# In the hybrid trunk, the second tiles of two forms of the pooled channels follow bank evictions on VectorE

## The chip, the cores and the metric

The kernel runs on one NeuronCore of a Trainium2 chip. The metric is the device time of one execution in microseconds (us); lower is better. TensorE (PE) multiplies matrices into the banks of PSUM, VectorE (DVE) and ScalarE (ACT) read the banks and work on tiles in SBUF, GpSimd (POOL) works on SBUF alone, and SyncE (SP), ScalarE and GpSimd issue DMAs. Each engine takes its own queue of instructions in a fixed order.

## The reference

One layer of a streaming encoder over 2048 positions of 1024 channels, and a final norm. What matters here is the first half of the layer:

```
xn = rmsnorm(x, norm1_g)
z  = xn @ w_in          # u_pool | q | f | i | o | branch gates
gates = sigmoid(zg + b_gate)                      # two of 1024 channels
ya = pool_mixer(u_pool, pool_w, pool_scale) @ w_pa    # 512 -> 1024 channels
yb = hgrn2_mixer(zq, zf, zi, zo, ...) @ w_pb          # a gated recurrence, 4 heads
merged = gates[0] * ya + gates[1] * yb
x = x + merged @ w_o
x = x + conv_glu_ffn(rmsnorm(x, norm2_g), ...)
out = rmsnorm(x, final_g)
```

The pool mixer takes trailing means over windows of 2, 4, 8 and 16 positions, multiplies each group of 128 channels by a matrix of its own and scales the result; these are the "pooled channels" that w_pa multiplies.

## The kernel before

**Passes and blocks.** The sequence is worked off in two passes of 1024 positions. A pass has a mixer (the projections, the pool mixer, the recurrence, the merge) and a feed-forward part. It works on two blocks of 512 positions at once, so that a tile has 128 channels and 512 positions.

**Seven products for eight.** Each large product is cut in a two by two manner: two halves of the contraction, two blocks of positions, two tiles of output channels. The eight partial products are made from seven (P1 to P7) by a Strassen-Winograd scheme. It multiplies sums of weights by sums of inputs. The sums of inputs are called forms: B11, B21, B22, T1 to T4. The table `FORM` says which product uses which: P1 B11, P6 T2, P5 T1, P7 T3, P2 B21, P4 T4, P3 B22, and `ORDER` is the order P1, P6, P5, P7, P2, P4, P3.

**Hi and lo.** Every operand is split into a high part (a cast on ScalarE) and a low part (what is left, a subtraction on VectorE), and each product is made of three matmuls: high by high, high by low, low by high. For weights this is done by the stream (lines 231 and 232), a few operands ahead of the products; for the forms by `split` (lines 659 and 660).

**A unit and its banks.** A `Unit` makes two output tiles for both blocks with three PSUM banks, X, Z and V. P1 and P2 add into X, P6, P7 and P4 into Z, P5 and P3 into V. Between two products of a bank its content has to be read: after P6 VectorE computes u2 from bank Z (line 1200), after P7 it computes u3 from bank Z (line 1204) and an output from bank V. P7's products can start only when u2 has read the bank, and P4's only when u3 has. `after("P6")` and `after("P7")` hand u2 and u3 to `first`, which remembers the latest of them. `second(ins)` puts an instruction behind the remembered one in the order of their engine; so far only the convolution of the feed-forward part uses it.

**The order of the work.** The Python program issues the matmuls in order. After every sixth matmul comes a tick, at which waiting tasks (generators) go on: the stream of weights, the four heads of the recurrence, the pool mixer and others. `yield n` waits n ticks. A planner then fixes the order of each engine's queue ahead of the run, from the program's order, from the dependencies and from estimated times; `in_turn` tells it that an instruction comes after the last matmul issued, `behind` that it comes after another instruction of its engine. Neither makes an engine wait for another engine on the chip.

**The pooled forms.** The mixer's last projection unit is the unit of gates 7 (tiles `gr_...` in the profile). Behind it come the products of the pooled channels with w_pa (tiles `pa_...`): two rounds d = 0, 1, in each of which two units (e = 0, 1) share the weights of a product, first all of unit 0's matmuls, then all of unit 1's. A form of the pooled channels has two tiles, j = 0 and 1 (two groups of 128 channels). `pa_task` (line 1460 on) makes them, paced by the counter `place`: it counts up behind each product of the last gate unit (1 after P1, 2 after P6, 3 after P5, 4 after P7 ... 7 after P3), and ahead of each product of the pooled units (8 at P1, 9 at P6, 10 at P5, 11 at P7, 12 at P2, 13 at P4, 14 at P3 of round 0). A product has twelve matmuls, so two ticks.

In `pa_task`, `minus` subtracts two tiles (line 1477), `form` splits the result. T2 (with t1 and t2, `mf_t` in the profile, and the parts `mf0T20h` to `mf0T21l` in the first pass) is issued from place 3 on, tile 0 at one tick and tile 1 at the next, both while P7 of the last gate unit is issued. T3's subtractions run on GpSimd, from place 5. T4 is issued from place 8, behind B21, tile 0 at one tick and tile 1 at the next, while P6 of the pooled units is issued. B22 (a negated copy on ScalarE, line 1519, and its split) is issued from place 10. In between, the heads of the recurrence issue `ss` and `st` (line 1118), `ot` (line 1139) on VectorE and `pv`, `po`, `pt` on TensorE.

Of the kernel before, what the change touches and what calls it, by code (L numbers as in the profile page):

```python
# [15 lines left out]
ALU = mybir.AluOpType  # L16
# [65 lines left out]
def tile_trunk(  # L82
# [26 lines left out]
    def slot(name, cols=TB, dt=F32):  # L109
        return slots.tile([P, cols], dt, tag="s", name=name, padded_shape=[P, 528])  # L110
# [148 lines left out]
    def behind(ins, other):  # L259

        tc.add_manual_dep(ins.ins, other.ins.name, mybir.DependencyInfo(
            mybir.DependencyClass.NoSync, mybir.DependencyReason.DATA), reason="behind")
# [7 lines left out]
    def second(ins):  # L270
        if urgent[0] is not None:
            behind(ins, urgent[0])
        return ins

    def in_turn(ins):

        tc.add_manual_dep(ins.ins, count[1].ins.name, mybir.DependencyInfo(
            mybir.DependencyClass.NoSync, mybir.DependencyReason.SCHED_ONLY), reason="in turn")

    stream = Stream()  # L280

    class Sums:
# [12 lines left out]
        def make(self, g):  # L295
            n = len(self.groups[g][0])
            for k in ("s1", "s2", "s3", "s4"):
                nm = f"{self.name}{g}{k}"
                self.t[g, k] = dram.tile([P, n, 512], F32, tag=nm, name=nm)
            for dst, src, add in (("s1", 2, 0), ("s3", 2, 0), ("s1", 3, 1), ("s3", 0, 1),  # L300
                                  ("s2", "s1", 0), ("s2", 0, 1), ("s4", "s2", 0), ("s4", 1, 1)):
                x = self.t[g, src] if isinstance(src, str) else self.groups[g][1][src]
                if add:
                    in_turn(pool.dma_start(self.t[g, dst], x, accum_op=ALU.add))
                else:
                    with tc.issue_after(stream.mark.ins):
                        act.dma_start(self.t[g, dst], x)
                yield SUM_LAG
            self.done.add(g)
# [343 lines left out]
    def split(src, name, on_pool=False):  # L653
        hi = slot(name + "h", TB, F32R)
        lo = slot(name + "l", TB, F32R)
        if on_pool:
            up = pool.tensor_scalar(hi, src, 1.0, 0.0, ALU.mult, ALU.add)
        else:
            up = act.copy(hi, src)
        low = dve.tensor_tensor(lo, src, f32(hi), ALU.subtract)  # L660
        last_split[0] = up, low
        return hi, lo
# [297 lines left out]
    def fetch(d, name, eng=sp):  # L960
        t = slot(name)
        eng.dma_start(t, d)  # L962
        return t


    def hgrn_task(b, h, d, q, vd, zd, od):
# [27 lines left out]
        def two_levels(hh):  # L994
# [27 lines left out]
            for i in range(0, NT, 2):  # L1022
                cc = slice(i, i + 2)
                mv = mvs[i]
                pa_ = bank(f"pl{b}_{h}_{hh}_{i}", 384)
                for c in range(2):
                    ins = pe.matmul(pa_[:, c * 192 : c * 192 + 192],  # L1027
                                    ks[:, (i + c) * P : (i + c + 1) * P],
                                    mv[:, c].rearrange("p s x -> p (s x)"),
                                    start=True, stop=True)  # L1030
                    if not (i or c):
                        in_turn(ins)
                ps = pa_.rearrange("p (c s x) -> p c s x", c=2, s=3)
                yield 1
                dve.copy_predicated(av[:, cc, :, 1, :], mask(hh, 2),
                                    ps[:, :, 0].rearrange("p c (b h) -> p c b h", h=hh))
                for t in range(2):
                    dve.copy_predicated(av2[:, cc, :, 1, :], mask(8 * hh + 1 - t, 2),
                                        ps[:, :, 1 + t].rearrange("p c (b h) -> p c b h", h=2 * hh))
# [12 lines left out]
        for lv in (0, 1, 2, 4, 6):  # L1052
# [7 lines left out]
            if lv < 2:  # L1060
                qd, ad = ((q1, ae), (q2, ao))[lv]
                if lv == 1:
                    act.copy(q2[:, :, 0].rearrange("p c (b h) -> p c b h", h=2), qv[:, :, :, 1, :])
                    yield AHEAD
                pa_ = bank(f"pl{b}_{h}_{hh}")
                for c in range(NT):
                    ins = pe.matmul(pa_[:, c * P : (c + 1) * P], ks[:, c * P : (c + 1) * P],
                                    qd[:, c].rearrange("p s x -> p (s x)"),
                                    start=True, stop=True)
                    if not c:  # L1070
                        in_turn(ins)
                yield 2
                pv4 = pa_.rearrange("p (c s x) -> p c s x", c=NT, s=2)
                dve.copy_predicated(ad, masks[-1 - lv].to_broadcast([P, NT, 64]), pv4[:, :, 1])
                pv4 = pv4[:, :, 0].rearrange("p c (b h) -> p c b h", h=hh)
            else:
                yield AHEAD
                pa_ = bank(f"pl{b}_{h}_{hh}", 256)
                for c in range(NT):
                    ins = pe.matmul(pa_[:hh, c * hh : (c + 1) * hh], ks[:, c * P : c * P + hh],  # L1080
                                    qv[:, c, 0, 1, :], start=True, stop=True)
                    if not c:
                        in_turn(ins)
                yield 2
                act.copy(av[:hh, :, 0, 1, :], pa_[:hh].rearrange("p (c h) -> p c h", c=NT))
# [285 lines left out]
    def mixer(b0, forms, late):  # L1371
# [90 lines left out]
        place = [0]  # L1462

        def pa_task():
            t = {}
            for hf, g in ((0, 0), (0, 1), (1, 0), (1, 2), (1, 1), (1, 3), (0, 2), (0, 3)):
                while (b0 + hf, g) not in md:
                    yield 1
                t[hf, g] = fetch(md[b0 + hf, g], f"mx{b0 + hf}_{g}")

            def form(key, j, x):
                pf[key].append(split(x, f"mf{b0}{key}{j}"))
                in_turn(last_split[0][0])

            def minus(key, j, x0, x1, eng=dve):
                x = slot(f"mf{b0}_{key}{j}")
                in_turn(eng.tensor_tensor(x, x0, x1, ALU.subtract))
                return x

            while place[0] < 2:  # L1480
                yield 1
            for j in range(2):
                form("B11", j, t[0, j])
                yield 1
            t1, t2 = [], []
            while place[0] < 3:
                yield 1
            for j in range(2):
                t1.append(minus("t1", j, t[1, j], t[0, j]))
                t2.append(minus("t2", j, t[1, j + 2], t1[j]))  # L1490
                form("T2", j, t2[j])
                yield 1
            while place[0] < 5:
                yield 1
            t3 = [minus("t3", j, t[1, j], t[1, j + 2], pool) for j in range(2)]
            for j in range(2):
                form("T1", j, t1[j])
                yield 1
            while place[0] < 6:
                yield 1  # L1500
            for j in range(2):
                form("T3", j, t3[j])
                yield 1
            while place[0] < 7:
                yield 1
            for j in range(2):
                form("B21", j, t[0, j + 2])
                yield 1
            while place[0] < 8:
                yield 1  # L1510
            for j in range(2):
                t4 = minus("t4", j, t[0, j + 2], t2[j])
                form("T4", j, t4)
                yield 1
            while place[0] < 10:
                yield 1
            for j in range(2):
                x = slot(f"mf{b0}_b22{j}")
                in_turn(act.activation(x, t[1, j + 2], AF.Copy, scale=-1.0))
                form("B22", j, x)  # L1520
                yield 1
# [3 lines left out]
        for n, (kind, i) in enumerate(PROJ):  # L1525
            if (kind, i) == ("u", 0):
                held["w"] = stream.get("pw")
            u = Unit(f"{kind[0]}r{b0}_{i}", "in", emits[kind](i))
            for p in ORDER:
                u.multiply(p, forms, late)  # L1530
                u.after(p)
                if n == len(PROJ) - 1:
                    if p == "P1":
                        quiet[0] = True
                        mtask = Task(pa_task())
                    place[0] += 1
# [437 lines left out]
```

## Time and profile before

| | before |
|---|---|
| median of 3 runs | 2515.26 us (2512.67 to 2516.94) |
| the profiled execution | 2514.4 us |
| its span, first to last instruction | 2512.7 us |
| mean granted clock of TensorE | 0.998 |
| TensorE busy, matmuls / weight loads | 2494.6 us / 2048.8 us |
| VectorE, ScalarE, GpSimd busy | 1996.1 / 1214.1 / 808.3 us |

In a timeline a row has the start and the duration in us, the engine, the line of the kernel, the operation, the tiles as out<-in, the shape and a count. Behind it, in brackets, is how long the engine had been idle and what released it. In the waits a row has the waiting engine and line, what it waited for, and then the total in us, the number of times and the longest. A view of windows has, for each stretch, its length, the busy time and count of PE, PEld, DVE, ACT and POOL, then the granted clock of TensorE, the share of the DMA engines and GB/s. The first pass's last gate unit and first pooled units lie at about 425 to 470 us, the second pass's at 1665 to 1715 us.

### The profile page before, as it was taken

How to read it: one execution, taken by the hardware profiler on the slowest of the kernel's cores; microseconds unless marked ns; L12 is line 12 of the kernel's file. 1: busy time of each engine (PE TensorE's matmuls, PEld its weight loads, DVE VectorE, ACT ScalarE, POOL GpSimd, SP SyncE). 2: the span in 40 equal slices, each digit the busy share in tenths (PEclk: the TensorE clock that was granted, in tenths of full speed). 3: DMA queues.
4: the chain of work that ended last, by engine and by line, in shares of the span. 5: the costliest groups of instructions: out<-in, count | busy, mean ns of one | idle time of the engine just before them, and what ended most of it. 6: DMA issues, size and time to landing. Idle time of an engine off the chain costs nothing.

```text
span 2512.7 us, 35696 instructions
## 1 busy us (share of the span) xinstructions
PE 2494.6 (99%) x11460; PEld 2048.8 (82%) x11460; DVE 1996.1 (79%) x3528; ACT 1214.1 (48%) x2286; POOL 808.3 (32%) x1139
## 2 busy tenths in 40 slices
PE   9999999999999999999999999999999999999998
PEld 7888888788888888888888888887888888888887
DVE  7788878897998778885596778778979888778755
ACT  5534443435555445553554434443355555445534
POOL 4343453403344333551320202123033433325410
PEclk9999999999999999999999999999999999999999
DMA  8877787687888789897344343446443444447852
GB/s 271 273 200 221 214 219 225 216 241 248 208 249 243 221 228 247 264 366 234 114 158 152 106 134 110 143 151 238 132 155 121 153 150 139 150 135 245 322 165 99
DMA packets 252332, 493.76 MB, mean 197 GB/s; under 512 B 26544, under 2 KB 43056, under 8 KB 251824
## 3 DMA queue, kind: packets, MB, share of 16 engines
q1 hardware_dynamic: 184512, 313.60, 38.4%
q0 software_dynamic: 42656, 112.74, 17.7%
q10 hardware_dynamic: 24976, 65.13, 7.5%
q8 instruction: 91, 1.49, 0.2%
q14 instruction: 97, 0.79, 0.1%
HBM read 381.79 MB, written 187.17 MB: 226 GB/s over the span
## 4 chain that ended last, share of the span: by engine, by line
PE 98%; DVE 1%; ACT 1%; DMA 0%; issue 0%; POOL 0%; SPq 0%; ACTq 0%
PE dn_P L148 17%; PE up_Z L148 15%; PE up_X L148 10%; PE up_V L148 10%; PE wo_P L148 6%; PE gr_Z L148 5%; PE gr_V L148 4%; PE pb L148 4%; PE gr_X L148 3%; PE io_Z L148 3%; PE fr_Z L148 3%; PE fr_V L148 2%; PE fr_X L148 2%; PE io_V L148 2%; PE pl L1027 2%; PE ur_Z L148 1%
## 5 line engine op out<-in xcount | busy, mean ns | idle before, releaser
L231 ACT CAST ops<-raw 128x512 fp32r<-128x512 f32 x794 | 490.1, 620 | 842.9 <-PE dn_P L148 176.4
L232 DVE TENSOR_TENSOR ops<-raw,ops 128x512 fp32r<-128x512 f32 x794 | 596.4, 755 | 206.2 <-ACT ops L231 199.4
L1705 DVE SCALAR_TENSOR_TENSOR e<-h,cols,e 128x512 f32<-128x512 f32 x176 | 141.4, 808 | 30.8 <-ACT e L1703 23.7
L1703 ACT ACTIVATE e<-h,cols 128x512 f32<-128x512 f32 x176 | 142.2, 814 | 25.6 <-DVE h L1160 18.3
L1708 DVE SCALAR_TENSOR_TENSOR e<-h,cols,e 128x512 f32<-128x512 f32 x176 | 134.9, 776 | 2.5
L962 POOL DMA_DIRECT2D g_P<-dg_P x154 | 83.7, 545 | 161.5 <-PE dn_P L148 111.6
L1273 POOL TENSOR_TENSOR gf_P<-e,e 128x512 f32<-128x512 f32 x44 | 61.7, 1403 | 150.2 <-DVE e L1714 95.9
L446 POOL TENSOR_TENSOR raw<-raw,raw 128x512 f32<-128x512 f32 x36 | 50.6, 1405 | 150.5 <-DVE ops L232 136.6
L1273 POOL TENSOR_TENSOR gf_P<-gf_P,e 128x512 f32<-128x512 f32 x44 | 59.2, 1345 | 71.7 <-DVE e L1714 71.2
L1698 POOL COPY h<-h 128x2 f32<-128x2 f32 x88 | 39.8, 465 | 117.7 <-DVE h L1159 110.9
L1413 POOL TENSOR_TENSOR q<-q,qs 128x512 f32<-128x512 f32 x16 | 21.8, 1363 | 167.5 <-ACT qs L1412 167.5
L1712 ACT ACTIVATE e<-e 128x512 f32<-128x512 f32 x88 | 55.6, 632 | 40.2 <-DVE e L1708 39.8
L1700 POOL COPY hist<-h 128x2 f32<-128x2 f32 x88 | 35.1, 398 | 116.7 <-DVE h L1160 114.7
L1160 DVE TENSOR_TENSOR h<-up_u,up_V 128x512 f32<-128x512 f32 x88 | 60.1, 683 | 10.2 <-PE up_V L148 9.7
L1248 DVE TENSOR_TENSOR x<-x,wo_P 128x512 f32<-128x512 f32 x88 | 55.9, 688 | 9.0 <-PE wo_P L148 8.6
L1248 DVE TENSOR_TENSOR ac<-ac,dn_P 128x512 f32<-128x512 f32 x72 | 47.2, 683 | 16.1 <-PE dn_P L148 15.8
L1012 POOL COPY qm<-q 128x64 f32<-128x64 f32 x64 | 26.6, 436 | 100.9 <-DVE q L1044 20.8
L1450 ACT ACTIVATE gt<-gt,cols 128x512 f32<-128x512 f32 x48 | 34.8, 725 | 49.9 <-DVE gt L1160 40.5
L1198 ACT COPY up_e<-up_X 128x512 f32<-128x512 f32 x44 | 25.8, 586 | 57.0 <-PE up_X L148 49.8
L1728 POOL DMA_DIRECT2D dg_P<-gf_P x88 | 50.7, 576 | 8.3 <-POOL gf_P L1273 7.4
L1698 POOL COPY h<-hist 128x2 f32<-128x2 f32 x88 | 44.4, 512 | 27.3 <-issue 14.8
L1027 PE MATMUL pl<-qm,k 128*128 128x192 f32 x256 | 50.2, 326 | 0.0
(1364 smaller groups left out, 8106.4 us busy)
## 6 DMA issues: line engine op xcount, KB each, us to landing
g_P<-dg_P POOLq DMA_DIRECT2D x154, 256.0 KB, 6.2
raw<-in_w_up_t SPq DMA_DIRECT2D x132, 256.0 KB, 3.2
raw<-in_w_in_t SPq DMA_DIRECT2D x98, 256.0 KB, 3.4
dg_P<-gf_P POOLq DMA_DIRECT2D x88, 256.0 KB, 3.9
dg_P<-e SPq DMA_DIRECT2D x66, 256.0 KB, 3.6
raw<-in_w_dn SPq DMA_DIRECT2D x66, 256.0 KB, 3.8
x<-in_x SPq DMA_DIRECT2D x64, 256.0 KB, 5.0
gd<-gt ACTq DMA_DIRECT2D x64, 256.0 KB, 3.0
```

The costliest lines, as they stand in the source:

```text
L148: count[1] = pe.matmul(*args, **kw)
L231: self.mark = act.copy(hi, v)
L232: low = self.low = dve.tensor_tensor(lo, v, f32(hi), ALU.subtract)
L962: eng.dma_start(t, d)
L1027: ins = pe.matmul(pa_[:, c * 192 : c * 192 + 192], ks[:, (i + c) * P : (i + c + 1) * P], mv[:, c].rearrange("p s x -> p (s x)"), start=Tru ...
L1160: return dve.tensor_tensor(dst, t, ps, ALU.add if how == "add" else ALU.subtract)
L1248: dve.tensor_tensor(t, t, ps[j], ALU.add if sg > 0 else ALU.subtract)
L1273: pin(eng.tensor_tensor(t, x0, x1, op))
L1698: pool.tensor_copy(h[:, 0:2], hist[:, mt] if hf == 0 else hs[s, 0][:, TB : TB + 2])
L1703: in_turn(act.activation(t, h[:, 2:], AF.Identity, bias=col(o_cb + mt), scale=col(o_cw + 4 * MF + mt)))
L1705: in_turn(second(dve.scalar_tensor_tensor(t, h[:, 1 : 1 + TB], col(o_cw + 2 * MF + mt), t, ALU.mult, ALU.add)))
L1708: dve.scalar_tensor_tensor(t, h[:, 0:TB], col(o_cw + mt), t, ALU.mult, ALU.add)
```

## The change

`in_turn` now returns its instruction. `minus` puts the second tile (j = 1) of t1 and of t4 behind the remembered eviction with `second`. The waits for a place become a helper, `reach`. The second tile of T2 (t1, t2 and the split) is issued at place 4 instead of 3, when u3 of the last gate unit is the remembered eviction. The second tile of T4 is issued at place 10, where it was issued one tick behind the first from place 8 on; the remembered eviction is then u2 of the pooled unit 1 in round 0. B22 is issued from place 11 instead of 10. T1, T3, B21, B11 and all first tiles keep their places. No instruction is added or taken away.

```diff
@@ def in_turn(ins)
         tc.add_manual_dep(ins.ins, count[1].ins.name, ...)
+        return ins
@@ def pa_task()
             def minus(key, j, x0, x1, eng=dve):
                 x = slot(f"mf{b0}_{key}{j}")
-                in_turn(eng.tensor_tensor(x, x0, x1, ALU.subtract))
+                ins = in_turn(eng.tensor_tensor(x, x0, x1, ALU.subtract))
+                if j and key in ("t1", "t4"):
+                    second(ins)
                 return x
 
-            while place[0] < 2:
-                yield 1
+            def reach(n):
+                while place[0] < n:
+                    yield 1
+
+            yield from reach(2)
...
             t1, t2 = [], []
-            while place[0] < 3:
-                yield 1
             for j in range(2):
+                yield from reach(3 + j)
                 t1.append(minus("t1", j, t[1, j], t[0, j]))
                 t2.append(minus("t2", j, t[1, j + 2], t1[j]))
                 form("T2", j, t2[j])
                 yield 1
...
-            while place[0] < 8:
-                yield 1
             for j in range(2):
+                yield from reach(8 + 2 * j)
                 t4 = minus("t4", j, t[0, j + 2], t2[j])
                 form("T4", j, t4)
                 yield 1
-            while place[0] < 10:
-                yield 1
+            yield from reach(11)
             for j in range(2):
                 x = slot(f"mf{b0}_b22{j}")
                 in_turn(act.activation(x, t[1, j + 2], AF.Copy, scale=-1.0))
```

More of the change, by code (lines that the diff above doesn't have):

```diff
@@ L1492, in pa_task @@
                 yield 1
-            while place[0] < 5:
-                yield 1
+            yield from reach(5)
             t3 = [minus("t3", j, t[1, j], t[1, j + 2], pool) for j in range(2)]
@@ L1498, in pa_task @@
                 yield 1
-            while place[0] < 6:
-                yield 1
+            yield from reach(6)
             for j in range(2):
@@ L1503, in pa_task @@
                 yield 1
-            while place[0] < 7:
-                yield 1
+            yield from reach(7)
             for j in range(2):
@@ L1508, in pa_task @@
                 yield 1
-            while place[0] < 8:
-                yield 1
             for j in range(2):
+                yield from reach(8 + 2 * j)
                 t4 = minus("t4", j, t[0, j + 2], t2[j])
@@ L1514, in pa_task @@
                 yield 1
-            while place[0] < 10:
-                yield 1
+            yield from reach(11)
             for j in range(2):
```

## The prediction

> **What bounds the kernel now.** I read the page first, then the waits of TensorE and of its weight loads, then the timelines of the stretches in which those waits lie. The page:
>
> ```profile
> span 2512.7 us, 35696 instructions
> PE 2494.6 (99%) x11460; PEld 2048.8 (82%) x11460; DVE 1996.1 (79%) x3528; ACT 1214.1 (48%) x2286; POOL 808.3 (32%) x1139
> PE 98%; DVE 1%; ACT 1%; DMA 0%; issue 0%; POOL 0%; SPq 0%; ACTq 0%
> ```
>
> TensorE carries 98% of the chain that ended last. Some 18 us of the span have no matmul in them (2512.7 - 2494.6), so a change that takes no matmul out can win no more than that and what slow matmuls cost. Where the holes are, the waits of TensorE say, and the same waits as its weight loads see them:
>
> ```profile
> PE pa_Z L148 <- DVE pa_u L1200: 4.1, 2, 2.1
> PE gr_Z L148 <- DVE gr_u L1204: 1.9, 2, 1.0
> ```
> ```profile
> PEld pa_Z L148 <- DVE pa_u L1200: 4.6, 2, 2.3
> PEld gr_Z L148 <- DVE gr_u L1204: 2.3, 2, 1.2
> ```
>
> Columns: total us, times, longest. Each wait occurs twice, once in each of the two passes over the sequence. In both, products into bank Z wait until VectorE has read that bank (u3 of the last gate unit, u2 of the second pooled unit). The timeline of VectorE in the first pass shows what stands ahead of u3:
>
> ```profile
> 434.64 1.03 DVE L660 TENSOR_TENSOR mf0T20l<-mf_t,mf0T20h 128x512 fp32r<-128x512 f32 x1 [0.43 <-ACT mf0T20h L659]
> 435.60 0.68 DVE L1477 TENSOR_TENSOR mf_t<-mx,mx 128x512 f32<-128x512 f32 x1
> 436.31 0.69 DVE L1477 TENSOR_TENSOR mf_t<-mx,mf_t 128x512 f32<-128x512 f32 x1
> 437.69 0.69 DVE L660 TENSOR_TENSOR mf0T21l<-mf_t,mf0T21h 128x512 fp32r<-128x512 f32 x1 [0.68 <-ACT mf0T21h L659]
> 438.30 0.68 DVE L1204 TENSOR_TENSOR gr_u<-gr_Z,gr_e 128x512 f32<-128x512 f32 x1
> ```
>
> The three instructions between T2's first low part and u3 are t1, t2 and the low part of the second tile, with a hole of 0.68 in which VectorE waits for the cast on ScalarE. TensorE beside it: the last product that u3 needs, and the wait.
>
> ```profile
> 432.69 0.39 PE L148 MATMUL gr_Z<-x_T33h,ops 128*128 128x512 f32 x1
> 439.04 0.50 PE L148 MATMUL gr_Z<-x_T40h,ops 128*128 128x512 f32 x1 [0.95 <-DVE gr_u L1204]
> ```
>
> u3's input was there at 433.1; it started 5.2 us later. The second place, VectorE and then TensorE:
>
> ```profile
> 452.86 0.68 DVE L660 TENSOR_TENSOR mf0T40l<-mf_t,mf0T40h 128x512 fp32r<-128x512 f32 x1
> 453.46 0.68 DVE L1200 TENSOR_TENSOR pa_u<-pa_e,pa_Z 128x512 f32<-128x512 f32 x1
> 454.05 1.12 DVE L1139 SCALAR_TENSOR_TENSOR ot<-po,ro,z 128x128 f32<-128x128 f32 x4
> 455.09 1.52 DVE L1477 TENSOR_TENSOR mf_t<-mx,mf_t 128x512 f32<-128x512 f32 x1
> 457.30 0.69 DVE L660 TENSOR_TENSOR mf0T41l<-mf_t,mf0T41h 128x512 fp32r<-128x512 f32 x1 [0.68 <-ACT mf0T41h L659]
> 457.91 0.68 DVE L1200 TENSOR_TENSOR pa_u<-pa_e,pa_Z 128x512 f32<-128x512 f32 x1
> ```
> ```profile
> 451.14 0.39 PE L148 MATMUL pa_Z<-mf0T21h,ops 128*128 128x512 f32 x1
> 454.58 0.40 PE L148 MATMUL pa_Z<-mf0T30h,ops 128*128 128x512 f32 x1
> 458.64 0.50 PE L148 MATMUL pa_Z<-mf0T30h,ops 128*128 128x512 f32 x1 [2.07 <-DVE pa_u L1200]
> ```
>
> Here t4 and the low part of T4's second tile, with the same hole of 0.68, stand ahead of the second u2, whose input was there at 451.5.
>
> **A third loss, behind the second wait.** In the second pass the products behind it run slowly. The busy time by stretches, the same 3.7 us behind the wait in both passes (the fraction ahead of the last two columns is the granted clock), and the first and the eleventh of the products that follow:
>
> ```profile
> 458.60:462.30 3.70, 3.66 (x16) 3.00 (x17) 3.17 (x5) 1.59 (x3) 0.54 (x1) 1.00 0.34 129
> 1703.70:1707.40 3.70, 3.64 (x9) 2.82 (x10) 3.18 (x6) 1.60 (x3) 0.52 (x1) 0.57 0.40 147
> ```
> ```profile
> 461.07 0.39 PE L148 MATMUL pa_X<-mf0B211l,ops 128*128 128x512 f32 x1
> ...
> 1701.13 0.60 PE L1145 MATMUL pt<-ident,ot 128*128 128x128 f32 x4
> 1703.76 0.51 PE L148 MATMUL pa_Z<-mf2T30h,ops 128*128 128x512 f32 x1 [2.03 <-DVE pa_u L1200]
> ...
> 1707.75 0.39 PE L148 MATMUL pa_X<-mf2B211l,ops 128*128 128x512 f32 x1
> ```
>
> Ten steps took 1707.75 - 1703.76 = 3.99 us there and 461.07 - 458.64 = 2.43 in the first pass: 1.56, or 1.6 us, lost to a granted clock of 0.57.
>
> **Part by part.**
>
> *T2's second tile* (t1, t2, cast, low part, in each pass) is issued one place later and behind u3. u3 can then start where t1 stood, at 435.60, and is done by 436.3. The product wants the bank where its weight load began to wait, 439.04 - 1.14 = 437.90 (half of the 2.3 above). The whole wait goes, with 1.6 us to spare. What is late next: nothing; the second tile comes some 1.3 us later than now (u3 and the gate's add ahead of it) and is first read at the P6 products of the pooled units:
>
> ```profile
> 448.61 0.40 PE L148 MATMUL pa_Z<-mf0T20h,ops 128*128 128x512 f32 x1
> ```
>
> That is 10 us after its low part ends now. Gain: 2.3 us over both passes.
>
> *T4's second tile* is issued behind the second u2. u2 then stands where t4 stood, at 455.09, and the bank is free at 455.09 + 0.68 + 0.05 = 455.82 (0.05 from u2's end at 458.59 to the product at 458.64). The weight load began to wait at 458.64 - 2.31 = 456.33. On the old clock the whole wait goes, 4.6 us over both passes. With the first wait gone TensorE comes 1.14 us earlier, though, at 455.19, and the first unit's P7, which today starts at 454.58 with its weight load 0.23 before, wants the first u2 by 453.21 where it is ready at 454.19 on the old clock. So VectorE must come earlier too. If it doesn't at all, 0.98 us a pass are given back at that first unit (the second then fits, 456.17 against 455.82). I take it that it does, since its feed is led by TensorE:
>
> ```profile
> ACT ops L231 <- PE gr_V L148: 1.3, 1, 1.3
> ACT ops L231 <- PE pa_X L148: 0.7, 1, 0.7
> ```
>
> These are ScalarE's waits from 440 to 462: its casts for the next weights start when TensorE releases a buffer, and the low parts ahead of u2 follow those casts. When TensorE is early, they are. So the sum keeps 4.6, and 4.6 - 2.0 is its lower bound.
>
> *The new wait.* t4 now queues behind u2 on VectorE, its cast on ScalarE and its low part behind t4. The whole chain takes 2.9 us now (455.09 to 457.99), so from 455.7 it ends at about 458.6, or 457.5 on the new clock if VectorE shifts. Its readers, and those of B22, which is issued one place later:
>
> ```profile
> 463.62 0.40 PE L148 MATMUL pa_Z<-mf0T41h,ops 128*128 128x512 f32 x1
> 465.70 0.39 PE L148 MATMUL pa_V<-mf0B220h,ops 128*128 128x512 f32 x1
> ```
>
> Both come 3.45 us earlier (1.14 + 2.31), at 460.2 and 462.2. T4 has 1.6 to 2.7 us to spare. B22 takes from 457.17 to 460.35 now:
>
> ```profile
> 457.17 0.62 ACT L1519 ACTIVATE mf_b<-mx 128x512 f32<-128x512 f32 x1
> 459.66 0.69 DVE L660 TENSOR_TENSOR mf0B221l<-mf_b,mf0B221h 128x512 fp32r<-128x512 f32 x1 [0.47 <-ACT mf0B221h L659]
> ```
>
> 3.2 us, to be done by 462.9, where its second tile is read (three products of 0.23 behind the first): it may start as late as 459.7 and be hidden. The evictions u3 and ya of the pooled units now share VectorE with T4 and B22 behind u2: ten instructions at the 0.6 us from start to start of the rows above, some 6 us from 455.8, as today, only in another order. No DMA is moved, and on GpSimd nothing but t3, in its old place. Cost: nothing within that cover, 0.98 us a pass if it fails as bounded above.
>
> How long t4 itself takes is open between 0.69 and 1.52: the same subtraction took 0.69 for the first tile, and 1.52 beside two GpSimd additions.
>
> ```profile
> 451.12 0.69 DVE L1477 TENSOR_TENSOR mf_t<-mx,mf_t 128x512 f32<-128x512 f32 x1
> 453.02 3.05 POOL L446 TENSOR_TENSOR raw<-raw,raw 128x512 f32<-128x512 f32 x2 [3.73 <-DVE ops L232]
> ```
>
> I keep 1.52, which the spare time above already holds.
>
> *The clock.* Without the second wait the slow ten steps go: 1.6 us in the profiled execution. It isn't certain for each execution: the first pass had the same wait and kept its clock at 1.00. The Trainium skill, in TensorE: Matmul & The Clock Gate, Part 1, says that the clock falls to half after an idle window of about 3.4 us, that the window runs freely, and its advice is to allow no gap over about 3 us. By that rule these gaps, of 2.6 us (1701.13 to 1703.76, transposes included), would cost no clock, and the sum would lack its 1.6 us; the row with 0.57 decides against it, and the free-running window would fit that only one of two equal gaps was hit. I keep the 1.6, with zero and twice it as its bounds.
>
> *Which row to sum.* By the matmul rows the two waits are 4.1 + 1.9 = 6.0, by the weight loads 4.6 + 2.3 = 6.9. I take the loads: matmuls of 0.39 start every 0.23, so the row of a matmul covers part of the hole behind it. [...]
>
> **Sum.** 2.3 + 4.6 + 1.6 = 8.5 us from the profiled execution's 2514.4 (span 2512.7, and 1.7 around it): 2505.9. The median of the three runs, 2515.26, lies 0.9 above that execution, so the forecast is 2506.8 us.
>
> **Rivals.**
>
> *VectorE doesn't come earlier.* For it: it is nearly full ahead of u2. Against it: ScalarE's two waits for TensorE. 2 x 0.98 is given back, and the clock saving may be absent as in the first pass: 8.5 - 2.0 - 1.6 = 4.9, so 2515.3 - 4.9 = 2510.4. Chance 0.15.
>
> *Only one place is cured.* The order of each engine is fixed ahead from estimated times, and an instruction of the recurrence (ot and its like) may land ahead of u2 or u3 in t4's stead. If the second wait stays, only 2.3 is won: 2513.0. Chance 0.08.
>
> *The change does nothing that counts*: the wait moves to the next bank eviction, 2515.3. For it: ten evictions and casts share VectorE there. Against it: the spare times above. Chance 0.05.
>
> *Slower: T4's second tile comes late.* Place: the P4 products of the first pooled units. t4 has to stand behind u2, but nothing says how far behind: it may be put behind the evictions of P7 and P2 as well. Deciding point: it starts later than 460.2 - 2.9 = 457.3 on the old clock. If it starts only when P4 is reached, TensorE waits for the whole chain of 2.9 and may run the slow clock behind it (1.6), in both passes: 2 x 4.5 = 9.0 lost against 8.5 won, 2515.8. ScalarE, which takes its queue in order, stood at this very cast before:
>
> ```profile
> ACT mf0T41h L659 <- DVE mf_t L1477: 3.3, 1, 3.3
> ```
>
> The casts of the next weights queue behind it; if they too come 2.9 late, 5.8 more, 2521.6. Chance 0.07, 0.04 of it with the weights.
>
> **How the numbers follow.** The forecast's chance is 0.65, the four rivals have 0.35. About 0.2%, 5.0 us, is what a measurement of this kernel can tell from no change; the three runs alone spread over 4.3 us. The low end is the forecast less a second clock loss saved (1.6) and 1.2 for the spread of the median: 2504.0. The high end takes in the first rival and half of the second with the same spread, 2512.5. Faster by over 0.2% means under 2510.2: nearly all of the forecast's cases and a part of the first rival, 0.68. Slower by over 0.2%: 0.04. The rest, 0.28, is within.
>
> **What would show it.** Right: no wait of gr_Z for u3 and of pa_Z for u2 among TensorE's waits, u3 directly behind T2's first low part, the second u2 ahead of the second t4, and a granted clock of 1.00 behind P7 in both passes. Wrong: a wait of pa_Z or pa_V for T4, B22 or u3; a wait of the first unit's P7 for u2 of up to 0.98 (first rival); or the same span with new waits elsewhere.

## The result and the profile after

| | before | after |
|---|---|---|
| median, 20 runs each | 2515.10 us (2512.67 to 2516.94) | 2510.89 us (2510.24 to 2513.03) |
| ratio, 95% interval | | 0.9985 [0.9979, 0.9991] |
| profiled execution, its span | 2514.4, 2512.7 us | 2511.74, 2510.0 us |

The change makes the kernel 4.2 us faster. The direction and the range were right, the forecast of 2506.8 was 4.1 us too low: half of the gain that was expected came. The interval of the ratio leaves 1 out, but the prediction had set 5.0 us as the line for a visible change, and 4.2 us fall in the part within that line, to which it gave 0.28. The page of the kernel after, its first two lines:

```profile
span 2510.0 us, 35693 instructions
PE 2495.4 (99%) x11460; PEld 2044.8 (81%) x11460; DVE 1997.8 (80%) x3528; ACT 1213.2 (48%) x2286; POOL 810.3 (32%) x1139
```

The engines do the same work as before. The waits of TensorE, and those of its weight loads (total us, times, longest):

```profile
PE pa_Z L148 <- DVE pa_u L1201: 0.9, 2, 0.5
PE wo_P L148 <- DVE x L1249: 0.7, 1, 0.7
PE pa_Z L148 <- DVE pa_u L1205: 0.5, 2, 0.3
```
```profile
PEld pa_Z L148 <- DVE pa_u L1205: 2.0, 4, 0.7
PEld pa_Z L148 <- DVE pa_u L1201: 1.7, 2, 0.9
```

The wait for u3 of the last gate unit (`gr_Z`) is gone, and so is round 0's wait for u2. Two smaller waits have come in their place: for round 1's u2 (line 1201 now, 1.7 us as the loads see it) and for the pooled units' u3 (line 1205, 2.0 us), 3.7 us in all. Where they lie, TensorE's rows in the first pass say; first of before, then of after.

```profile
462.92 0.39 PE L148 MATMUL pa_Z<-mf0T40h,ops 128*128 128x512 f32 x1
...
464.33 0.40 PE L148 MATMUL pa_Z<-mf0T40h,ops 128*128 128x512 f32 x1
...
476.75 0.39 PE L148 MATMUL pa_Z<-mf0T30h,ops 128*128 128x512 f32 x1
```
```profile
453.27 0.39 PE L148 MATMUL pa_Z<-mf0T30h,ops 128*128 128x512 f32 x1
...
455.01 0.48 PE L148 MATMUL pa_Z<-mf0T30h,ops 128*128 128x512 f32 x1
...
459.33 0.50 PE L148 MATMUL pa_Z<-mf0T40h,ops 128*128 128x512 f32 x1
...
461.25 0.50 PE L148 MATMUL pa_Z<-mf0T40h,ops 128*128 128x512 f32 x1 [0.26 <-DVE pa_u L1205]
...
474.45 0.51 PE L148 MATMUL pa_Z<-mf0T30h,ops 128*128 128x512 f32 x1 [0.47 <-DVE pa_u L1201]
```

P7 of the pooled unit 0 starts at 453.27 (454.58 before) and P7 of unit 1 at 455.01 (458.64 before), neither behind a wait. At P4 of unit 0 TensorE is 3.59 us earlier than before (459.33 against 462.92); the prediction had 3.45. Then the gain shrinks: 3.08 at P4 of unit 1, which waits for u3, and 2.30 at P7 of round 1, which waits for u2. So 1.29 us a pass are given back within 15 us. VectorE in these 15 us, first the rows of before that the prediction doesn't show, then after:

```profile
458.51 0.69 DVE L660 TENSOR_TENSOR mf0B220l<-mf_b,mf0B220h 128x512 fp32r<-128x512 f32 x1
...
460.27 0.68 DVE L1204 TENSOR_TENSOR pa_u<-pa_Z,pa_e 128x512 f32<-128x512 f32 x1
...
461.60 0.68 DVE L1204 TENSOR_TENSOR pa_u<-pa_Z,pa_e 128x512 f32<-128x512 f32 x1
...
472.50 3.18 DVE L232 TENSOR_TENSOR ops<-raw,ops 128x512 fp32r<-128x512 f32 x2
475.60 1.27 DVE L1200 TENSOR_TENSOR pa_u<-pa_e,pa_Z 128x512 f32<-128x512 f32 x2
```
```profile
453.38 0.67 DVE L1201 TENSOR_TENSOR pa_u<-pa_e,pa_Z 128x512 f32<-128x512 f32 x1
453.98 0.68 DVE L232 TENSOR_TENSOR ops<-raw,ops 128x512 fp32r<-128x512 f32 x1
454.58 0.68 DVE L1478 TENSOR_TENSOR mf_t<-mx,mf_t 128x512 f32<-128x512 f32 x1
455.95 1.01 DVE L661 TENSOR_TENSOR mf0T41l<-mf_t,mf0T41h 128x512 fp32r<-128x512 f32 x1 [0.69 <-ACT mf0T41h L660]
457.14 1.54 DVE L661 TENSOR_TENSOR mf0B220l<-mf_b,mf0B220h 128x512 fp32r<-128x512 f32 x1 [0.17 <-ACT mf0B220h L660]
458.60 0.67 DVE L1205 TENSOR_TENSOR pa_u<-pa_Z,pa_e 128x512 f32<-128x512 f32 x1
...
459.92 0.68 DVE L661 TENSOR_TENSOR mf0B221l<-mf_b,mf0B221h 128x512 fp32r<-128x512 f32 x1
460.51 0.68 DVE L1205 TENSOR_TENSOR pa_u<-pa_Z,pa_e 128x512 f32<-128x512 f32 x1
...
466.59 3.50 DVE L232 TENSOR_TENSOR ops<-raw,ops 128x512 fp32r<-128x512 f32 x3
...
470.61 3.18 DVE L232 TENSOR_TENSOR ops<-raw,ops 128x512 fp32r<-128x512 f32 x2
473.72 1.27 DVE L1201 TENSOR_TENSOR pa_u<-pa_e,pa_Z 128x512 f32<-128x512 f32 x2
```

The second u2 stands ahead of t4, as intended, at 453.38 (457.91 before). But the low parts of T4 and B22 now stand between t4 and u3, and two of them take 1.01 and 1.54 us. So u3 of unit 0 starts 1.67 us earlier than before (458.60 against 460.27), where TensorE is 3.59 us earlier: the 2 us by which u3 was early in before (done at 460.95, P4 at 462.92) are used up. Later, five low parts of weights take 3.50 and 3.18 us ahead of round 1's u2; the last two took 3.18 us in before too, where u2 was still in time. GpSimd works beside these:

```profile
454.74 3.38 POOL L447 TENSOR_TENSOR raw<-raw,raw 128x512 f32<-128x512 f32 x2 [5.81 <-DVE ops L232]
...
462.94 6.00 POOL L1588 TENSOR_TENSOR ya<-ya,gl 128x512 f32<-128x512 f32 x4
470.23 1.31 POOL L447 TENSOR_TENSOR raw<-w135s,raw 128x512 f32<-128x512 f32 x1 [1.29 <-DVE ops L232]
471.50 1.75 POOL L1588 TENSOR_TENSOR ya<-ya,gl 128x512 f32<-128x512 f32 x1
```

The same 21 us by windows, before and then after (PE, PEld, DVE, ACT, POOL, clock, DMA):

```profile
453.00:474.00 21.00, 18.93 (x84) 15.24 (x83) 18.73 (x26) 7.19 (x14) 13.29 (x10) 1.00 0.47 160
```
```profile
453.00:474.00 21.00, 20.71 (x90) 16.01 (x88) 19.93 (x25) 8.74 (x16) 15.13 (x10) 1.00 0.57 179
```

VectorE was busy for 18.73 of 21 us and is now busy for 19.93: in this order, and with its instructions stretched beside GpSimd, it has little room left to follow a faster TensorE. Its u2 of round 1 starts only 1.88 us earlier than before (473.72 against 475.60), while TensorE had been 3.1 to 3.6 earlier.

The clock behind the second pass's P7, after:

```profile
1700.40:1704.10 3.70, 3.70 (x19) 3.06 (x18) 2.84 (x4) 3.33 (x6) 3.06 (x2) 1.00 1.05 391
```

It stays at 1.00, where before had 0.57.

**The account.** Two stretches of each pass can be measured by starts of the same matmuls in all kernels: *gate*, from a P6 matmul of the last gate unit to the first P1 matmul of the pooled units, and *pooled*, from there to a fixed matmul of the recurrence's output product. *Rest* is the sum of seven long stretches behind them in both passes (1787 us), in which the change touches nothing and the order of the instructions on each engine is the same in both kernels.

| us | gate, passes 1 and 2 | pooled 1 | pooled 2 | rest |
|---|---|---|---|---|
| before | 23.25, 23.21 | 67.54 | 74.16 | 1787.26 |
| before, a second profile | 23.24, 23.23 | 67.53 | 74.14 | 1787.27 |
| after | 22.03, 22.01 | 66.72 | 71.68 | 1789.25 |
| after, a second profile | 22.03, 22.01 | 66.72 | 71.70 | 1789.30 |

The changed stretches win 1.22 + 1.20 + 0.82 + 2.48 = 5.7 us, and the rest loses 2.0. (In the first profile of after about 1 us more goes at the wait for `wo_P` at 577 us, 100 us behind the change; the second profile doesn't have it.)

### The profile page after: what moved, and what is told of

Its sections match the earlier page's. It is cut to its first block, busy times and chain, and to the rows that moved or that the text cites. A ratio compares the mean times of both kernels' runs of the same rounds, so it can differ in the third digit from the quotient of the medians.

```text
span 2510.0 us, 35693 instructions
## 1 busy us (share of the span) xinstructions
PE 2495.4 (99%) x11460; PEld 2044.8 (81%) x11460; DVE 1997.8 (80%) x3528; ACT 1213.2 (48%) x2286; POOL 810.3 (32%) x1139
## 4 chain that ended last, share of the span: by engine, by line
PE 95%; DVE 3%; ACT 1%; issue 1%; DMA 0%; POOL 0%; SPq 0%; ACTq 0%; DVEq 0%
PE dn_P L148 17%; PE up_Z L148 15%; PE up_V L148 10%; PE up_X L148 10%; PE wo_P L148 5%; PE gr_Z L148 5%; PE pb L148 4%; PE gr_V L148 3%; PE gr_X L148 3%; PE io_Z L148 3%; PE fr_Z L148 3%; PE fr_V L148 2%; PE fr_X L148 2%; PE io_V L148 2%; PE pl L1028 2%; PE ur_Z L148 1%
```

## The experiments

The theories, with their letters in the expectations. *The order on VectorE* (A): both waits are cured, and each pass then gives back what stands ahead of u3 and of round 1's u2 on a VectorE that is full. *Only one place is cured*, a rival of the prediction. *The clock* (E): what is won or lost is mostly slow matmuls behind a gap. And, for the part outside, *the place of the tiles* (F): the rest runs at another pace in each program.

**T2 alone and T4 alone.** Each keeps one half of the change. Only the main lines of the diffs are shown here.

```diff
 t2_only:
-                yield from reach(8 + 2 * j)
+                yield from reach(8)
-                if j and key in ("t1", "t4"):
+                if j and key in ("t1",):
-            yield from reach(11)
+            yield from reach(10)
 t4_only:
-                yield from reach(3 + j)
+            yield from reach(3)      # ahead of the loop's body
-                if j and key in ("t1", "t4"):
+                if j and key in ("t4",):
```

> T2's part alone: T2's second tile behind u3 as in the changed kernel, T4 and B22 as before. Theory A (the waits went as forecast, and VectorE, which has no idle time from u2 of round 0 to u2 of round 1, gives part of it back later): gr_Z's wait of 1.0 to 1.2 goes in both passes, pa_Z's wait for u2 stays at 2.0 to 2.3, the time is 2.0 to 2.6 us under the kernel before. Theory B (VectorE's backlog, not TensorE, sets when u2 comes): pa_Z's wait grows to 3.2 to 3.5 as TensorE comes early to it, and the time is within 0.6 of the kernel before.

> T4's part alone: T4's second tile behind u2 and B22 one place later as in the changed kernel, T2 as before. Theory A: gr_Z's wait of 1.0 to 1.2 stays, the wait for u2 goes, and as TensorE comes 1.2 later to the pooled units than in the changed kernel there is less for VectorE to give back at P4 and in round 1: the time is 2.5 to 4.5 under the kernel before. Theory C (what was won in the mixer is lost far behind it, as the planner puts other instructions in other places): little is left, within 1.5 of the kernel before.

Measured: T2 alone 2511.28 us (2508.94 to 2513.99), ratio 0.9988 [0.9979, 0.9997]; T4 alone 2510.8 (2510.57 to 2511.82), 0.9988 [0.9979, 0.9997]; before beside them 2514.22. T2 alone is 2.9 us under before, a little more than expected; T4 alone is 3.4 under, within what was expected. The waits of T2 alone and of T4 alone:

```profile
PE pa_Z L148 <- DVE pa_u L1201: 3.9, 2, 2.0
```
```profile
PE gr_Z L148 <- DVE gr_u L1205: 2.0, 2, 1.0
...
PE pa_Z L148 <- DVE pa_u L1201: 0.6, 2, 0.3
```

Each half cures its own wait and leaves the other, so both places are cured by the whole change. In stretches, T2 alone wins 1.22 a pass in *gate*, 0.08 in *pooled 1* (67.46) and nothing in *pooled 2* (74.17, with the slow clock behind the wait as in before). T4 alone wins 1.62 in *pooled 1* (65.92). The whole change wins 1.22 + 0.82 = 2.04, not 1.30 + 1.62 = 2.92: the halves don't add, since VectorE follows one of them and not both. By the medians alone the halves can't be told from the whole, and T2 alone spreads over 5 us.

**B22 later.** If B22's low parts are what delays u3, they should be issued behind it. The first try moves B22 one place on; the second does that and, too, holds the low parts of the weights behind the remembered u2 from round 1's P6 on (until P5), and while P6 is issued the stream converts two operands ahead in place of four.

```diff
 b22_at12, both:
-            yield from reach(11)
+            yield from reach(12)
 both, in the loop over rounds and products, and where the stream converts weights:
+                if (d, p) == (1, "P6"):
+                    stream.room, hurry[0] = LOOKAHEAD - 2, True
...
+            if hurry[0]:
+                second(low)
```

> The changed kernel with B22 issued from place 12 in place of 11, so that the planner puts u3 of both pooled units ahead of B22's low parts on VectorE. Theory A: the new wait of P4 for u3 (0.5 to 0.7 a pass by the leads of TensorE) goes, but the same work then stands ahead of round 1's u2, whose wait of 0.7 to 0.8 stays or grows: 0 to 1.2 under the changed kernel, so 4.2 to 5.4 under the kernel before. Rival D (VectorE is no bound, the order of B22 alone is): the whole 1.3 a pass comes back, 6.5 to 7 under the kernel before.

> The changed kernel with B22 from place 12 and, in round 1, the low parts of the two weight operands that stand ahead of u2 on VectorE put behind it. Theory A: neither P4 nor round 1's P7 waits, 1.0 to 2.6 under the changed kernel, so 5.2 to 6.8 under the kernel before, unless the weights come late in their turn. Theory C: no more than 4.2 under the kernel before, since the loss lies behind the mixer.

Measured: 2512.28 us (2510.67 to 2515.52), ratio 0.9994 [0.9985, 1.0003], and 2513.4 (2511.64 to 2516.74), 0.9996 [0.9987, 1.0005]: a miss. The waits of the first:

```profile
PE pa_V L148 <- DVE mf0B221l L661: 0.9, 1, 0.9
PE pa_V L148 <- ACT mf0B221h L660: 0.8, 1, 0.8
```

P4's wait for u3 is gone, as the theory has it, but P3 now waits for B22's second tile, first for its cast and then for its low part (the rows are of the first pass, the second has the same). VectorE:

```profile
459.75 0.74 DVE L661 TENSOR_TENSOR mf0B220l<-mf_b,mf0B220h 128x512 fp32r<-128x512 f32 x1
...
464.58 0.68 DVE L661 TENSOR_TENSOR mf0B221l<-mf_b,mf0B221h 128x512 fp32r<-128x512 f32 x1
```

P3 has used up the first tile at 462.9. The cast of the second, which now stands behind weights' casts on ScalarE, lets it go on at 463.9, and the low part, which stands behind weights' low parts on VectorE, only at 465.3. This is the late form that the prediction feared as its slower rival, in B22's place instead of T4's, and it shows how narrow the slot is: place 11 comes too early for u3, place 12 too late for P3.

**The second profile of after, and a stall of known size.** Five or twelve additions of 128x512 tiles into unused tiles are put on VectorE ahead of round 0's second u2.

```diff
+                    idle = None
+                    if (d, p, e) == (0, "P6", 1):
+                        hi, lo = pf["B11"][0]
+                        for _ in range(5):       # 12 in the other kernel
+                            idle = in_turn(dve.tensor_tensor(slot(f"junk{b0}_{_}"), f32(hi), f32(lo), ALU.add))
                     units[e].after(p)
+                    if idle is not None:
+                        behind(urgent[0], idle)
```

> The changed kernel once more, beside the kernel before. Expected by all theories: 3.6 to 4.8 under the kernel before. If the clock gate takes part in the kernel before (theory E: a gap of 2.3 to 2.6 us at P7 costs another 1.6 us when the gate's free-running window lies over it), the times of the kernel before spread over 3 us or more and those of this one over less, as this one has no gap of that length.

> The changed kernel with five additions on VectorE, of no use, right ahead of the second u2 of round 0 in each pass: 3.0 us of VectorE work where t4, cast and low part stood. By the spare time in the changed trace (u2 done 0.7 ahead of its need) the wait for u2 comes back at about 2.3 us. Theory E: over the two passes the time rises by 4.6 and, in those executions where the window lies over the gap, by 1.6 more for each, so the times spread over 1.5 to 3 us; 4.6 to 7.8 over the changed kernel. Without the clock: 4.6 in all executions, or less where VectorE later has slack.

> The same with twelve additions, 7.2 us of VectorE work ahead of u2: the wait is about 6.5 us in each pass. Theory E: no position of the window is free of such a gap, so the clock is halved behind both waits, 1.6 to 3.2 us lost for each, on top of 13.0: 16 to 19 us over the changed kernel, and the granted clock behind both waits is 0.5 to 0.6. Without the clock: 13.0 over the changed kernel and a granted clock of 1.00.

Measured: after again 2511.15 us (2510.35 to 2512.05), ratio 0.9988 [0.9979, 0.9997], with before beside it at 2514.33. Five additions 2518.3 (2517.42 to 2519.03), 1.0015 [1.0006, 1.0024], 7.2 over after. Twelve 2524.31 (2524.15 to 2525.24), 1.004 [1.0028, 1.0053], 13.2 over after. The wait of the kernel with twelve, the first product behind it and the clock there, in the first pass:

```profile
PE pa_Z L148 <- DVE pa_u L1201: 12.2, 2, 6.1
```
```profile
461.23 0.80 PE L148 MATMUL pa_Z<-mf0T30h,ops 128*128 128x512 f32 x1 [6.09 <-DVE pa_u L1201]
...
463.95 0.63 PE L148 MATMUL pa_X<-mf0B210h,ops 128*128 128x512 f32 x1
...
464.67 0.40 PE L148 MATMUL pa_X<-mf0B210h,ops 128*128 128x512 f32 x1
```
```profile
461.20:464.90 3.70, 3.67 (x9) 2.93 (x10) 3.13 (x5) 3.03 (x6) 2.37 (x2) 0.55 0.00 0
```

Waits of 6.1 us slow the clock in both passes. By the eight steps from 461.23 to 464.67, 3.44 us instead of 8 x 0.23 = 1.84, the first pass loses 1.6; thirteen such steps in the second (1711.83 to 1717.39) lose 2.6. Waits and clock make 16.4. The stretches grew by 6.55 and 7.51 (*pooled* 73.27 and 79.19), 14.1 in all, and the medians by 13.2. What is missing in the stretches, 2.3, is about the 2 x 1.29 that the kernel after gives back at u3 and at round 1's u2: with TensorE late there, neither wait is left. So the waits that remain in after are slack that VectorE regains whenever TensorE is held up before them, which is the order on VectorE again, from the other side. The expectation had left this out and was too high.

The kernel with five waits 4.5 us for u2, over four times, and slows the clock in the second pass alone, as before does. There the slow clock costs next to nothing: *pooled 2* grows by 3.1 and *pooled 1* by 3.0 (74.77 and 69.69), as a slower TensorE finds less of the later waits (its loads wait 0.2 us for u3 there and 1.9 in the first pass).

The clock does change between executions of one kernel. Of the 21 executions of before beside these, three had a mean granted clock of 1.000 and took 2512.8 to 2513.3 us, three had 0.998 and took 2514.7 to 2515.7. Before spreads over 3.3 us there and after over 1.7, as expected if the clock takes part in before.

**GpSimd out of the way.** The multiplications of the pooled outputs by their gates on GpSimd are left out, so this kernel computes the outputs without these gates.

```diff
-                pool.tensor_tensor(t, t, g, ALU.mult)
```

> The changed kernel without the multiplications of the pooled outputs by their gates on GpSimd (six for each round and pass; the outputs lack those gates). Theory A, with the stretch of VectorE's instructions beside GpSimd as its cause: low parts of 1.2 to 1.9 in round 1 fall to 0.6 to 0.7, VectorE reaches round 1's u2 2 us or more earlier, and that wait of P7 (0.47 by the matmul row) goes; P4's wait for u3 stays, as it lies ahead of the first such multiplication. If the order alone is the cause, both waits stay.

Measured: 2509.0 us, one run. Its waits, and VectorE at round 1:

```profile
PE pa_Z L148 <- DVE pa_u L1205: 0.6, 2, 0.3
```
```profile
465.15 1.89 DVE L232 TENSOR_TENSOR ops<-raw,ops 128x512 fp32r<-128x512 f32 x3
...
467.56 2.29 DVE L232 TENSOR_TENSOR ops<-raw,ops 128x512 fp32r<-128x512 f32 x2
469.77 0.68 DVE L1201 TENSOR_TENSOR pa_u<-pa_e,pa_Z 128x512 f32<-128x512 f32 x1
```

The three low parts that took 3.50 us take 1.89, the two that took 3.18 take 2.29, and round 1's wait for u2 is gone; P4's wait for u3, which has other GpSimd work beside it, stays. *Pooled 1* takes 66.08, 0.64 less than in after. So round 1's part of what is given back comes of VectorE's instructions being stretched beside GpSimd.

**The rest of the kernel, and the cure.** Before again; a kernel that differs from after by one small write on GpSimd at the end of the first mixer; B22's low parts, alone, held behind the remembered u3 while its casts keep their place; and this together with the weights held behind round 1's u2.

```diff
 pad:
+        if not b0:
+            pool.memset(slot("pad")[:, :1], 0.0)
 b22_low, best (best has the edits of `hurry` above as well):
-                form("B22", j, x)
-                yield 1
+                in_turn(act.copy(hi, x))
+                yield 1
+                second(in_turn(dve.tensor_tensor(lo, x, f32(hi), ALU.subtract)))
```

> The kernel before, profiled a second time. Theory F (away from the changed stretch the cadence of TensorE belongs to a program, by where its tiles lie, since the order of all instructions there is the same in both programs): the five long stretches away from it take what they took in its first profile within 0.3 us each (254.9, 208.0, 420.3, 425.5 and 212.6; 255.3, 208.2, 420.7, 425.7 and 213.1 in both profiles of the changed kernel, 1.7 us more in all). Rival G (chance of a run): they scatter by 0.5 us or more. The clock may or may not be halved behind P7, by theory E.

> The changed kernel with one more tile taken from the pool of slots and let go at the end of the first mixer (a memset of one column on GpSimd writes it), so that every later tile lies one slot further on; the order of all other instructions is the same. Theory F: up to that place the stretches are those of the changed kernel within 0.1 us, behind it they differ by 0.2 to 1 us each and the time by up to 2 us either way. Rival G: nothing but the scatter of runs, within 0.5 us of the changed kernel, 3.2 to 4.2 under the kernel before.

> The changed kernel with B22's copies and casts on ScalarE at their places, but its two low parts on VectorE one tick later and behind the u3 issued before them. Theory A: P4 no longer waits for u3 (0.55 a pass in TensorE's leads), B22 isn't late (it was late by 2.1 a pass where its copies moved to place 12 as well); round 1's wait for u2 stays at 0.5 to 0.8. So the stretch of the pooled units takes 66.2 in place of 66.7 us, 1 us in all under the changed kernel if the rest stays. If VectorE's total is all that counts, the wait of round 1 grows by what P4 saves, and nothing is won.

> The same, and in round 1 the low parts of two weight operands behind u2 on VectorE. Theory A: no wait for u3 or u2 in the pooled units is left, their stretch takes 65.4 to 65.6 us in the first pass, 2.2 to 2.6 us in all under the changed kernel, so 6 us under the kernel before, plus or minus the 1 to 2 us that theory F gives to any program.

Measured, with before at 2515.18 beside them: before again 2515.08 (2513.27 to 2516.4), ratio 1.0001 [0.9993, 1.001]; the small write 2510.25 (2509.13 to 2511.59), 0.9983 [0.9974, 0.9992]; B22's low parts 2510.25 (2509.52 to 2511.7), 0.9982 [0.9973, 0.9991]; with the weights 2509.15 (2508.06 to 2512.03), 0.9977 [0.9968, 0.9986]. The waits of the last two for a bank of the pooled units: B22's low parts alone leave

```profile
PE pa_Z L148 <- DVE pa_u L1201: 1.1, 2, 0.6
```

and the last kernel has none. Its VectorE:

```profile
456.38 1.02 DVE L664 TENSOR_TENSOR mf0T41l<-mf_t,mf0T41h 128x512 fp32r<-128x512 f32 x1 [0.69 <-ACT mf0T41h L663]
457.32 0.68 DVE L1208 TENSOR_TENSOR pa_u<-pa_Z,pa_e 128x512 f32<-128x512 f32 x1
...
458.64 0.68 DVE L1527 TENSOR_TENSOR mf0B220l<-mf_b,mf0B220h 128x512 fp32r<-128x512 f32 x1
...
472.61 1.28 DVE L1204 TENSOR_TENSOR pa_u<-pa_e,pa_Z 128x512 f32<-128x512 f32 x2 [2.00 <-ACT pa_e L1202]
```

u3 stands ahead of B22's low parts (the first takes 0.68 there, the second 1.72 at 460.57, where nothing waits for it), and round 1's u2 now waits for its input. Over the 21 us from 453 VectorE is busy for 18.24, less than in before, though TensorE is faster: it was full in after by the order, and by GpSimd beside it, not by the amount of its work. The *pooled 1* stretch is 66.17 with the first edit and 65.33 with both, 0.55 and 1.39 less than after: about the 0.51 and 0.78 that TensorE's rows showed as given back. So the order on VectorE is shown as the cause, at both places, and the kernel with both edits is the fastest here that computes the whole layer: 6.0 us under before, as expected, and by its interval [0.9968, 0.9986] not told apart from after.

The rest of the kernel stays: *rest* is 1788.66 with the small write, 1789.21 and 1789.33 in the last two, against 1787.27 in before again.

## Why the prediction was half right

- **Both waits are cured: right.** u3 of the gate unit went at 435.50, where the prediction put it at 435.60, and *gate* fell by 1.22 and 1.20 (1.14 each predicted). The second u2 no longer stands behind t4, and until P4 of unit 0 TensorE had won 3.59 us (3.45 predicted). The weight loads were the better rows to sum: *gate* fits their 1.14 better than the 0.95 of the matmul row. T2's and T4's second tiles were late for nobody.
- **"VectorE must come earlier too ... I take it that it does": right at the place it was asked of.** The first unit's u2 started at 451.75, 1.71 earlier than before, and P7 of unit 0 didn't wait. The first rival's time of 2510.4 nearly fits the result by luck: its 2 x 0.98 are lost at P7 of unit 0, where nothing was lost, and it has the clock's 1.6 as not won, which was won. Its reason, a VectorE that is nearly full, holds further on.

```profile
451.75 0.68 DVE L1201 TENSOR_TENSOR pa_u<-pa_e,pa_Z 128x512 f32<-128x512 f32 x1
```

- **The step that failed** is the last one of the new wait: "ten instructions at the 0.6 us from start to start ... some 6 us from 455.8, as today, only in another order. ... Cost: nothing within that cover". The order counted. Before, T4's low part and both of B22's ran ahead of u3 too, the last two at 458.51 and 459.66, but TensorE came from its wait for u2 only at 458.64 and to P4 at 462.92, 2 us after u3 was done. With that wait gone TensorE comes 3.6 us sooner, u3 only 1.7, and the low parts of T4 and B22 ahead of it decide when P4 starts. Nor did they take 0.6: two of them took 1.01 and 1.54 beside GpSimd, with 0.69 and 0.17 of waiting for casts before them. The prediction had such a row before it (t4's 1.52 beside GpSimd) and applied it to t4 alone. And it stopped at P3 of round 0, where round 1's P7 needs the same VectorE 12 us later. Cost by the rows: 0.51 + 0.78 = 1.29 a pass, 1.4 by the stretches (3.45 - 2.04), 2.8 in all, where the sum had zero. A wait of pa_Z for u3 was one of the prediction's own signs of being wrong.
- **The clock's 1.6: right for the profiled execution.** *Pooled 2* fell by 2.48 where *pooled 1* fell by 0.82, which is 1.66 more. Both profiles of before have the slow steps in the second pass, neither of after has any. Waits of 2.0 us are enough for it there and not in the first pass, whose wait was the same. The Trainium skill, TensorE: Matmul & The Clock Gate (What's actually happening), has the window of about 3.4 us run freely; the traces agree, and show which of two equal gaps is hit (last section). Its advice (Why this matters for your kernels) to have no gap of over about 3 us is too generous here, by the 0.57 in the prediction's row and by 0.59 in the second profile of before.
- **Nothing in the sum stood for the rest of the kernel**, which lost 2.0 us with the same instructions in the same order. This is nearly as large as the loss at the step that failed, and isn't explained.

The sum for the profiled executions: 8.5 - 2.8 - 2.0 = 3.7 us; the second profile of after lies 2514.4 - 2510.5 = 3.9 under before's.

## What to carry to other kernels

When a wait is taken away, the engine that caused it loses the time in which it caught up. So follow that engine's queue on, beyond the cured place, to the next evictions that it owes, and count each instruction ahead of them with the duration that it has beside its neighbours, not with its shortest. Moving a piece of work out of the way of one eviction puts it in the way of the next; what helped here was to split it, with the casts early and only the last step held behind the eviction.

## What the runs showed of the hardware

**VectorE beside GpSimd.** A 128x512 subtraction of two SBUF tiles takes 0.68 to 0.69 us alone, and 1.01 and 1.54 us in the rows above where GpSimd adds such tiles beside it (1.52 for t4 in before). One that reads a bank of PSUM and one SBUF tile keeps its 0.67 to 0.69 (u3 at 460.51, with GpSimd busy from 460.13 for 1.60). The Trainium skill, SBUF — State Buffer (Who interferes with whom), says that `tensor_tensor` with both inputs in SBUF contends with GpSimd's reads and one with a single SBUF input doesn't. The rows agree.

**The half clock lies on a grid.** In the record of the granted clock, half clock comes in pieces of 3.41 us (longer ones stand at the very end of the program, behind the last matmuls): from 1704.22 in before, 1704.39 in its second profile, 1702.51 in T2 alone and 1706.28 with five additions; with twelve it lasts 6.83 us, twice 3.41, from 457.68 and from 1710.37. In one execution the starts lie whole steps of 3.413 us apart (367 steps from 457.68 to 1710.37; 497 from 7.80, a slow piece at the start of before, to 1704.22), and the place of this grid against the program differs between executions. In the first four of these executions the gap at P7 without any matmul is 1.9 to 2.1 us long in both passes. The four gaps of the second passes lie wholly between two marks of the grid (1701.73 to 1703.76 between 1700.81 and 1704.22 in before), and half clock follows from the next mark on. The four of the first passes have a mark within them (456.57 to 458.64, with a mark at 458.36), and none follows. So in these traces a gap of this length costs the clock or not by its place in the grid, and what one execution loses isn't what the next one does.

**A pace that belongs to the program.** *Rest* came to 1787.26 and 1787.27 in the two profiles of before and to 1789.25 and 1789.30 in those of after, though nothing in it differs. All other kernels lie between 1788.1 (T4 alone) and 1790.3 (five additions). The small write took 0.6 us off it, which shows that such a shift needs no work to speak of. The shift has no wait of its own in the trace, and it isn't spread evenly: of some 8100 steps from one matmul's start to the next in the rest, about 2700 differ by 5 ns or more between before and after, up or down and nearly all by less than 20, and the 2 us are what is left of their sum. Between the two profiles of before 14 do. Ahead of the change, from 20 to 420 us, at most some 50 of 2000 steps differ between before and after. The kernel with the small write keeps the steps of after until just behind its write at 612.8 us, and from 640 us on up to half of them differ by 5 ns or more, though all other instructions run in the same order. A shift in time alone doesn't do that: the two profiles of after lie 1 us apart from 577 us on, and 37 of their 8100 steps differ. The write takes one tile more, so that later tiles may lie elsewhere. This points to the place of the tiles, but no run tried that by itself, and the cause stays open. For small changes it sets a floor of some 2 us under what a sum of waits can foretell.
